# Pooling mixer: the mixer's weights first, on raw inputs, then the norm's scale, then the pooling

## The chip, the core and the metric

The kernel runs on one core of one Trainium2 chip. The metric is the device time of one execution in microseconds (us), the median of several runs. The core's engines are TensorE (PE in the profile, with PEld for its weight loads), VectorE (DVE), ScalarE (ACT), GpSimd (POOL), and SyncE (SP), which here issues the DMA transfers. Each works through its own queue in program order, and semaphores make one wait for another.

## The reference

A trunk of two layers on 512 tokens of 1024 features, in float32: pooling mixer, gated MLP, sliding-window attention, gated MLP, each behind an RMSNorm, with plain residual adds. The change is in the pooling mixer of layer 0, the first thing the kernel computes:

```python
def rms_norm(x, g):
    y = xf * lax.rsqrt(jnp.mean(xf * xf, axis=-1, keepdims=True) + RMS_EPS)
    return (y * g.astype(jnp.float32)).astype(x.dtype)

def pool_mixer(h, w, b, scale):
    csum = jnp.cumsum(hf, axis=1)
    for gi, win in enumerate(POOL_WINDOWS):          # 2, 4, 8, 16; 256 features each
        ...
        count = jnp.minimum(t1, win)
        mean = (c - lo) / count                       # causal mean over win tokens
        outs.append(mean - hf[..., sl])
    y = jnp.einsum('bsgc,gcd->bsgd', p, w) + b        # 256 x 256 weights a group
    return y.reshape(B, S, D) * scale

    h = h + mix                                       # then rms_norm and the gated MLP
```

## The kernel before

Tokens are handled in 4 tiles of 128 (`NT`), features in 8 chunks of 128 (`NC`), two chunks to each pooling window. In the residual `h` the features lie on the partitions and the 512 tokens along the row, one tile per chunk. PSUM has eight banks of 512 float32 columns. Products in nearly full precision are made of three fp32r matmuls (`mm3`, L84 to L86): an operand x is split into a rounded part, `x_h`, which ACT writes, and the rest, `x_l`, which DVE writes (`split_scaled`, L258 and L259, with a factor for each feature); weights are split in the same manner (L98 on ACT, L101 on DVE or POOL). A few matmuls take plain float32 operands.

The mixer comes in these steps:

1. SP loads the inputs token-major (`xt<-x_tok`, L145), the mixer's weights (L149), the vectors (L150), three weight tiles of the MLP (L90), and the inputs once more, feature-major, as `h` (L318).
2. TensorE multiplies zeros (`warm`, L270) while nothing has arrived.
3. For each token tile, ACT squares and sums the inputs (L288; for the first tile DVE does half, L277), a short chain on ACT and DVE gives the norm's factor for each token (`rsqrt_mean`, L193 to L211), and DVE multiplies the pooling band by it (`sband`, L297). The band is a small matrix, 128 x 144, that has 1/window in the places of the window and -1 more on the diagonal; the first tile has a variant for the first tokens (`edge`). Eight float32 matmuls (L299) then pool that tile, with the scale in the band, into eight banks, feature-major.
4. `mixed` (order letter m) splits each bank with the norm's gain into `px_h`, `px_l`; `product` (p) multiplies by the weights, 6 matmuls for each chunk; `bias` (b, L338) adds bias times scale to `h`; `total` (t, L341) adds the scaled product to `h`.
5. `normed` (n) splits `h` with the next norm's gain into `f0x_h` and `f0x_l`, the operands of MLP 0; `early_weights` (w) splits the MLP's first weight tiles, the l part on POOL in quarters; `norm.add` sums the squares of `h` (ACT L222, POOL L231) for the MLP's norm, whose statistics (`ones` against `n_acc`, L237) are used behind the first four weight tiles.

`pin` keeps what it wraps in program order on its engine; the order string near L348 sets that order for the last three groups of steps. The MLP begins with two weight tiles together: for each chunk k there are six matmuls, so that chunk k+1 is needed 6 matmuls after chunk k; then come two more tiles over all eight chunks, the second's statistics in between, and so on.

Of the kernel before, what the change touches and what calls it, by code (L numbers as in the profile page):

```python
# [54 lines left out]


@with_exitstack
def trunk(ctx: ExitStack, tc: tile.TileContext, x_tok, x_t, vecs, w_pool, w_kq, w_v, w_o, w_in, w_out, out_a, out_b):
    nc = tc.nc
    V, A, G, T = nc.vector, nc.scalar, nc.gpsimd, nc.tensor  # L60
    PSUM = bass.MemoryType.PSUM
# [7 lines left out]
    def small(pool, n, words, dt=F32, **kw):  # L69
        return pool.tile([P, words], dt, **kw)[:, :n]  # L70
# [76 lines left out]
    wpool_raw = [fst.tile([P, 1024], F32, name=f"wpool{g}_raw") for g in range(2)]  # L147
    for g in range(2):
        nc.sync.dma_start(wpool_raw[g], w_pool[:, g * 1024 : (g + 1) * 1024])  # L149
    nc.sync.dma_start(vec, vecs)  # L150
    h = [xp.tile([P, S], F32, tag="h", name=f"h{c}") for c in range(NC)]

    def col(i):
        return vec[:, i : i + 1]
# [2 lines left out]
    ident = cst.tile([P, P], F32, name="ident")  # L157
    make_identity(nc, ident)


    rc = small(fst, 16, 64, name="rc")
    for t in range(15):
        V.memset(rc[:, t : t + 1], 1.0 / (t + 1))
    band = fst.tile([P, 8, BW], F32, name="band")
    def edge_copy(g):
        a = WINDOWS[g] - 1
        pin(V.tensor_copy(band[:, 4 + g, a:], band[:, g, a:]))

    for g, w in enumerate(WINDOWS):
        b = band[:, g, :]  # L170
        V.memset(b, 1.0 / w)
        G.affine_select(b, b, [[1, BW]], ALU.is_ge, 0.0, base=0, channel_multiplier=-1)
        G.affine_select(b, b, [[-1, BW]], ALU.is_ge, 0.0, base=w - 1, channel_multiplier=1)
        G.affine_select(b, b, [[1, BW]], ALU.not_equal, 1.0 / w - 1.0, base=0, channel_multiplier=-1)
        f = band[:, 4 + g, : w - 1]
        G.affine_select(f, rc[:, : w - 1], [[1, w - 1]], ALU.is_ge, 0.0, base=0, channel_multiplier=-1)
        G.tensor_tensor(f, f, ident[:, : w - 1], ALU.subtract)
        if g < 2:
            edge_copy(g)
    ones = cst.tile([P, P], F32, name="ones")  # L180
    G.memset(ones, 1.0)


    def rsqrt_mean(dst, ssq, n, root=False):


        def tmp(k, dt=F32):
            return small(sm, n, 16, dt, tag=f"rs_{k}", name=f"rs_{k}", bufs=4)

        v = tmp("v")  # L190
        y = tmp("y")
        if root:
            A.activation(y, ssq, AF.Sqrt, bias=eps, scale=1.0 / D)  # L193
            pin(V.tensor_scalar(v, ssq, -0.5 / D, -0.5 * EPS, ALU.mult, ALU.add))
            pin(V.reciprocal(y, y))
        else:
            V.tensor_scalar(v, ssq, 1.0 / D, EPS, ALU.mult, ALU.add)
            sh = tmp("i", I32)
            V.tensor_scalar(sh, v.bitcast(I32), 1, None, ALU.logical_shift_right)
            V.tensor_scalar(y.bitcast(I32), sh, -1.0, float(0x5F3759DF), ALU.mult, ALU.add)  # L200
            V.tensor_scalar(v, v, -0.5, None, ALU.mult)
        t = tmp("t")
        steps = 1 if root else 3
        for it in range(steps):
            z = dst if it == steps - 1 else y
            if n == 1:
                V.scalar_tensor_tensor(t, y, y, v, ALU.mult, ALU.mult)
            else:
                V.tensor_tensor(t, y, y, ALU.mult)
                V.tensor_tensor(t, t, v, ALU.mult)  # L210
            V.scalar_tensor_tensor(z, t, 1.5, y, ALU.add, ALU.mult)  # L211
# [48 lines left out]
        return xh, xl  # L260


    def pool_mixer(norm, xs, ws):
        r0 = small(fst, NT, 32, name="r0")
        ss0 = small(fst, 2 * NT, 32, name="ss0")

        warm = small(fst, BW, 192, name="warm")
        V.memset(warm, 0.0)
        for i in range(12):
            T.matmul(banks[-1][:, :BW], lhsT=warm[:, :P], rhs=warm, start=True, stop=True)  # L270
        for i in range(NT):

            cut = D // 2 if i == 0 else D
            junk = fst.tile([P, D], F32, tag="junk", name=f"junk{i}")
            if cut < D:
                pin(
                    V.tensor_tensor_reduce(  # L277
                        out=junk[:, cut:],
                        in0=xt[:, i, cut:],
                        in1=xt[:, i, cut:],  # L280
                        scale=1.0,
                        scalar=0.0,
                        op0=ALU.mult,
                        op1=ALU.add,
                        accum_out=ss0[:, NT : NT + 1],
                    )
                )
            A.activation(junk[:, :cut], xt[:, i, :cut], AF.Square, accum_out=ss0[:, i : i + 1])  # L288
            if cut < D:
                pin(V.tensor_tensor(ss0[:, i : i + 1], ss0[:, i : i + 1], ss0[:, NT : NT + 1], ALU.add))  # L290
                for g in (2, 3):
                    edge_copy(g)
            rsqrt_mean(r0[:, i : i + 1], ss0[:, i : i + 1], 1, root=True)
            n = min(BW, S - i * P)
            sband = fst.tile([P, 4, BW], F32, tag="sband", name=f"sband{i}", bufs=2)
            e = 0 if i else 4
            pin(V.tensor_scalar(sband[:, :, :n], band[:, e : e + 4, :n], r0[:, i : i + 1], None, ALU.mult))  # L297
            for c in range(NC):
                T.matmul(  # L299
                    banks[c][:, i * P : i * P + n],  # L300
                    lhsT=xt[:, i, c * P : (c + 1) * P],
                    rhs=sband[:, c // 2, :n],
                    start=(i == 0),
                    stop=(i == NT - 1),
                    skip_group_check=True,
                )
        wpool = []
        for g in range(4):
            raw = wpool_raw[g // 2][:, (g % 2) * 512 : (g % 2 + 1) * 512]
            hh = fst.tile([P, 512], F32R, name=f"wpool{g}_h")  # L310
            ll = fst.tile([P, 512], F32R, name=f"wpool{g}_l")
            A.activation(hh, raw, AF.Copy)
            pin(V.tensor_tensor(ll, raw, hh.bitcast(F32), ALU.subtract))
            wpool.append((hh, ll))
        pre = [(0, 1), (0, 0), (1, 1), (1, 0)]
        raws = [fetch(w_in[0, j, t], D, f"wi0_{j}_{t}") for j, t in pre[:3]]
        for c in range(NC):
            nc.sync.dma_start(h[c], x_t[:, c, :])  # L318
        bs = small(cst, NC, 64, name="bs")
        pin(V.tensor_tensor(bs, vec[:, V_PB : V_PB + NC], vec[:, V_PS : V_PS + NC], ALU.mult))  # L320
        pool_x = {}

        def mixed(c):
            pool_x[c] = split_scaled(banks[c], col(V_NM + c), f"px{c}", pin)

        def early_weights(i):
            ws.append(in_weights(0, *pre[i], G, raws[i] if i < 3 else None, pin))

        def product(c):
            g = c // 2  # L330
            ps = bank("ps")
            for k in range(2):
                w = tuple(t[:, k * 256 + (c % 2) * P :][:, :P] for t in wpool[g])
                mm3(ps, w, pool_x[2 * g + k], k == 0, k == 1)
            return ps

        def bias(c):
            pin(A.activation(h[c], h[c], AF.Identity, bias=bs[:, c : c + 1]))  # L338

        def total(c):  # L340
            pin(V.scalar_tensor_tensor(h[c], ps[c], col(V_PS + c), h[c], ALU.mult, ALU.add))  # L341

        def normed(c):
            xs.append(split_scaled(h[c], col(V_NFF + c), f"f0x{c}", pin))


        ps = {}
        order = (  # L348
            "m0 m1 p0 p1 w0 m2 m3 p2 p3 b0 b1 t0 m4 m5 p4 p5 t1 b2 b3 t2 m6 m7 p6 p7 t3 w1 b4 b5 t4 t5 "
            "n0 b6 b7 t6 n1 t7 n2 w2 n3 n4 w3 n5 n6 n7"  # L350
        )
        for step in order.split():
            c = int(step[1])
            if step[0] == "p":
                ps[c] = product(c)
            else:
                {"m": mixed, "b": bias, "t": total, "n": normed, "w": early_weights}[step[0]](c)
        for c in range(NC):
            norm.add(c)

# [472 lines left out]
```

## Time and profile before

| | us |
|---|---|
| median of 3 runs (lowest, highest) | 927.53 (927.15, 928.12) |
| the profiled execution | 929.0 |
| its span, first to last instruction | 926.9 |
| TensorE busy in it | 913.3 |
| first matmul of MLP 0 | 27.52 |

The times of instructions below are counted from the start of the span. A row of a timeline has the start, the duration (from the start of the first to the end of the last where several are joined, "x6"), engine, line, operation, output<-inputs, shape and, in brackets, the idle time ahead of it with what ended it. A row of a group has the count and, behind the bar, busy us and mean ns of one, then the engine's idle time ahead. A row of one tile has the shortest, median and longest duration in ns, then the first and last start. A row of windows has its length, PE's busy time with the number of matmuls, the granted clock, the DMA engines' share and GB/s. Instructions next to each other on one engine overlap a little at their ends. One float32 matmul is two records.

### The profile page before, as it was taken

How to read it: one execution, taken by the hardware profiler on the slowest of the kernel's cores; microseconds unless marked ns; L12 is line 12 of the kernel's file. 1: busy time of each engine (PE TensorE's matmuls, PEld its weight loads, DVE VectorE, ACT ScalarE, POOL GpSimd, SP SyncE). 2: the span in 40 equal slices, each digit the busy share in tenths (PEclk: the TensorE clock that was granted, in tenths of full speed). 3: DMA queues.
4: the chain of work that ended last, by engine and by line, in shares of the span. 5: the costliest groups of instructions: out<-in, count | busy, mean ns of one | idle time of the engine just before them, and what ended most of it. 6: DMA issues, size and time to landing. Idle time of an engine off the chain costs nothing.

```text
span 926.9 us, 11709 instructions
## 1 busy us (share of the span) xinstructions
PE 913.3 (99%) x4419; PEld 769.2 (83%) x4419; DVE 577.8 (62%) x974; ACT 422.9 (46%) x682; POOL 132.6 (14%) x216
## 2 busy tenths in 40 slices
PE   8999999999999999999999999999999999999997
PEld 7888888888888888898888888888888888888896
DVE  6589766336777754455887472987743377677433
ACT  7765443223444443436887451744422244444532
POOL 3800000000000001217665040000000000000022
PEclk9999999999999999999999999999999999999999
DMA  8233222343222223322110041242233423322312
GB/s 332 71 113 114 94 84 79 94 128 113 92 91 95 75 77 101 130 91 91 47 46 24 20 140 52 85 152 92 63 94 100 136 91 94 109 80 64 94 62 91
DMA packets 28855, 88.13 MB, mean 95 GB/s; under 512 B 3200, under 2 KB 4352, under 8 KB 28800
## 3 DMA queue, kind: packets, MB, share of 16 engines
q1 hardware_dynamic: 28800, 87.40, 29.1%
q8 instruction: 34, 0.56, 0.2%
q14 instruction: 21, 0.17, 0.1%
HBM read 85.29 MB, written 2.10 MB: 94 GB/s over the span
## 4 chain that ended last, share of the span: by engine, by line
PE 88%; POOL 3%; ACT 3%; DVE 2%; issue 2%; DMA 1%; SPq 0%; ACTq 0%; POOLq 0%; DVEq 0%
PE bank L84 29%; PE bank L85 29%; PE bank L86 29%; POOL wi_l L101 2%; DMA wi_raw<-w_in 1%; ACT sc L625 1%; POOL n_acc L231 1%; PE bank L608 1%; PE bank L638 1%; POOL wo_l L101 0%; DVE q L521 0%; DVE tl L642 0%; PE bank L248 0%; DVE wi_l L101 0%; ACT th L641 0%
## 5 line engine op out<-in xcount | busy, mean ns | idle before, releaser
L98 ACT ACTIVATE wi_h<-wi_raw 128x1024 fp32r<-128x1024 f32 x88 | 93.0, 1060 | 102.0 <-PE bank L85 94.2
L231 POOL TENSOR_TENSOR n_acc<-n_acc,n_sq 128x512 f32<-128x512 f32 (+1 forms) x28 | 37.2, 1328 | 706.3 <-ACT n_sq L222 699.5
L84 PE MATMUL bank<-f0x_h,wi_h 128*128 128x512 f32 x352 | 137.2, 390 | 0.0
L85 PE MATMUL bank<-f0x_l,wi_h 128*128 128x512 f32 x352 | 137.2, 390 | 0.0
L84 PE MATMUL bank<-f1x_h,wi_h 128*128 128x512 f32 x352 | 137.1, 390 | 0.0
L84 PE MATMUL bank<-zh,wo_h 128*128 128x512 f32 (+1 forms) x363 | 137.0, 378 | 0.0
L86 PE MATMUL bank<-f0x_h,wi_l 128*128 128x512 f32 x352 | 137.0, 389 | 0.0
L86 PE MATMUL bank<-f1x_h,wi_l 128*128 128x512 f32 x352 | 136.9, 389 | 0.0
L85 PE MATMUL bank<-f1x_l,wi_h 128*128 128x512 f32 x352 | 136.9, 389 | 0.0
L86 PE MATMUL bank<-zh,wo_l 128*128 128x512 f32 (+1 forms) x363 | 136.6, 376 | 0.0
L85 PE MATMUL bank<-zl,wo_h 128*128 128x512 f32 (+1 forms) x363 | 136.6, 376 | 0.0
L101 DVE TENSOR_TENSOR wi_l<-wi_raw,wi_h 128x1024 fp32r<-128x1024 f32 x84 | 103.6, 1236 | 50.2 <-ACT wi_h L98 48.4
L98 ACT ACTIVATE wo_h<-wo_raw 128x768 fp32r<-128x768 f32 (+1 forms) x70 | 57.5, 823 | 121.8 <-PE bank L85 109.8
L365 DVE TENSOR_TENSOR c_u<-bank,n_rb 128x512 f32<-128x512 f32 x88 | 60.0, 687 | 76.6 <-PE bank L86 76.4
L101 DVE TENSOR_TENSOR wo_l<-wo_raw,wo_h 128x768 fp32r<-128x768 f32 (+1 forms) x66 | 60.3, 914 | 54.5 <-ACT wo_h L98 54.3
L85 PEld LDWEIGHTS bank<-zl,wo_h 128*128 128x128 f32 x363 | 68.3, 188 | 12.4
L84 PEld LDWEIGHTS bank<-zh,wo_h 128*128 128x128 f32 x363 | 68.3, 188 | 12.4
L86 PEld LDWEIGHTS bank<-zh,wo_l 128*128 128x128 f32 x363 | 68.3, 188 | 12.4
L85 PEld LDWEIGHTS bank<-f0x_l,wi_h 128*128 128x128 f32 x352 | 66.1, 188 | 14.6 <-DVE f0x_l L259 0.8
L85 PEld LDWEIGHTS bank<-f1x_l,wi_h 128*128 128x128 f32 x352 | 66.1, 188 | 13.8
L86 PEld LDWEIGHTS bank<-f1x_h,wi_l 128*128 128x128 f32 x352 | 66.1, 188 | 13.7
L84 PEld LDWEIGHTS bank<-f0x_h,wi_h 128*128 128x128 f32 x352 | 66.1, 188 | 13.7
(175 smaller groups left out, 1482.6 us busy)
## 6 DMA issues: line engine op xcount, KB each, us to landing
wi_raw<-w_in SPq DMA_DIRECT2D x88, 512.0 KB, 3.2
wo_raw<-w_out SPq DMA_DIRECT2D x31, 384.0 KB, 3.1
wo_raw<-w_out SPq DMA_DIRECT2D x31, 320.0 KB, 2.9
kq_raw<-w_kq SPq DMA_DIRECT2D x10, 512.0 KB, 3.2
wo_raw<-w_o SPq DMA_DIRECT2D x8, 512.0 KB, 3.2
xt<-x_tok SPq DMA_DIRECT2D x4, 512.0 KB, 5.2
h<-x_t SPq DMA_DIRECT2D x8, 256.0 KB, 8.6
wpool_raw<-w_pool SPq DMA_DIRECT2D x2, 512.0 KB, 8.4
```

The costliest lines, as they stand in the source:

```text
L84: T.matmul(ps, lhsT=wh, rhs=xh, start=start, stop=False, **kw)
L85: T.matmul(ps, lhsT=wh, rhs=xl, start=False, stop=False, **kw)
L86: T.matmul(ps, lhsT=wl, rhs=xh, start=False, stop=stop, **kw)
L98: pin(A.activation(h[:, :n], raw[:, :n], AF.Copy))
L101: (eng or V).tensor_tensor(l[:, o], raw[:, o], h[:, o].bitcast(F32), ALU.subtract)
L231: eng.tensor_tensor(self.acc[:, lo:hi], self.acc[:, lo:hi], sq[:, lo:hi], ALU.add)
L365: V.tensor_tensor(u, ps, rb, ALU.mult)
L608: T.matmul(o, lhsT=qt, rhs=kt[:, kk : kk + 256], start=x == 0, stop=x == 1)
L625: A.activation(t, t, AF.Exp, bias=neg[:, i : i + 1], scale=-1.0, accum_out=den[:, i : i + 1])
L638: T.transpose(ps[:, i * P : (i + 1) * P], sc[i // 2][:, i % 2, kb * P : (kb + 1) * P], ident)
```

## The change

Pooling (over tokens), the mixer's weights (over features) and the norm's scale (for each token) can be applied in another order. After the change the weights come first, on raw inputs:

- There is no token-major copy. SP loads `gm` (the norm's gain, 4 KB), then `h` and the weights in turns of 256 KB (lines 152 to 157 of the new program).
- `scaled` (w) multiplies the weights by the norm's gain on ACT and DVE. `mix` (y) multiplies, with the inputs as stationary operand, so the result has tokens on the partitions: y0 to y2 are 24 float32 matmuls of 256 columns, y3 is 24 fp32r matmuls of three-part products. They fill eight banks with two token tiles each, 256 columns for a tile.
- `square` (s) sums the squares on ACT and DVE; `scales` (r) gets all four factors by 4 float32 matmuls with `ones` and one scalar chain.
- `evict` (e) applies the factor to each token tile while it splits: `yh` on ACT, `yl` on DVE, 32 pieces of 256 columns. `pool` (c) multiplies these by the band in fp32r: 9 matmuls for each chunk, feature-major, into the same banks.
- `bias` of chunks 0 to 3 is done by POOL. `total` (L385) and `normed` (L268, L269) compute what they did.
- The order string is rewritten, and so is the order on the engines.

SP's queue at its start, before and now:

```order
-L145 DMA xt<-x_tok 128x1024 x4
-L149 DMA wpool_raw<-w_pool 128x1024 x2
-L150 DMA vec<-vecs 128x692
+L867 UNCONDITIONAL_BRANCH
+L152 DMA gm<-vecs 128x8
+L154 DMA h_95<-x_t 128x512
+L155 DMA wpool_raw<-w_pool 128x512
+L156 DMA h_96<-x_t 128x512
```

The four 512 KB tiles of the token-major input are gone, and `h`, which stood behind the third weight tile of the MLP, comes first.

VectorE from the last mixer operands to the MLP's operands. `h_96` to `h_103` are the eight chunks in before; this is before:

```order
L341 SCALAR_TENSOR_TENSOR h_99<-bank_73,vec,h_99 128x512
L341 SCALAR_TENSOR_TENSOR h_100<-bank_74,vec,h_100 128x512
L341 SCALAR_TENSOR_TENSOR h_101<-bank_75,vec,h_101 128x512
L259 SCALAR_TENSOR_TENSOR f0x_l<-h_96,vec,f0x_h 128x512
L341 SCALAR_TENSOR_TENSOR h_102<-bank_70,vec,h_102 128x512
L259 SCALAR_TENSOR_TENSOR f0x_l<-h_97,vec,f0x_h 128x512
L341 SCALAR_TENSOR_TENSOR h_103<-bank_71,vec,h_103 128x512
L259 SCALAR_TENSOR_TENSOR f0x_l<-h_98,vec,f0x_h 128x512
L259 SCALAR_TENSOR_TENSOR f0x_l<-h_99,vec,f0x_h 128x512
```

The totals (L341) stand several chunks ahead of the splits (L259). The same place of VectorE now, where the chunks are `h_95` to `h_102`:

```order
L385 SCALAR_TENSOR_TENSOR h_95<-bank_70,vec,h_95 128x512
L269 SCALAR_TENSOR_TENSOR f0x_l<-h_95,vec,f0x_h 128x512
L348 SCALAR_TENSOR_TENSOR yl_429<-bank_77,r_207,yh_428 128x256 x2
L348 SCALAR_TENSOR_TENSOR yl_429<-bank_76,r_207,yh_428 128x256 x2
L385 SCALAR_TENSOR_TENSOR h_96<-bank_71,vec,h_96 128x512
L269 SCALAR_TENSOR_TENSOR f0x_l<-h_96,vec,f0x_h 128x512
L385 SCALAR_TENSOR_TENSOR h_97<-bank_72,vec,h_97 128x512
L269 SCALAR_TENSOR_TENSOR f0x_l<-h_97,vec,f0x_h 128x512
```

The first total and split stand ahead of the last group's evictions, and then total and split take turns.

ScalarE in before, from the mixer's splits to the MLP's (L258 with a bank writes `px_h`, with `h` writes `f0x_h`):

```order
L258 ACTIVATE px_h<-bank_76,vec 128x512
L258 ACTIVATE px_h<-bank_77,vec 128x512
L98 ACTIVATE wi_0_0_h<-wi_0_0_raw 128x1024
L338 ACTIVATE h_100<-h_100,bs 128x512
L338 ACTIVATE h_101<-h_101,bs 128x512
L258 ACTIVATE f0x_h<-h_96,vec 128x512
L338 ACTIVATE h_102<-h_102,bs 128x512
L338 ACTIVATE h_103<-h_103,bs 128x512
L258 ACTIVATE f0x_h<-h_97,vec 128x512
```

ScalarE now, with the waits that each instruction carries (DVE_49 and PE_49 are the semaphores that VectorE and TensorE count up):

```order
L347 ACTIVATE yh_394<-bank_74,r_207 128x256
L347 ACTIVATE yh_394<-bank_74,r_207 128x256 [waits DVE_49]
L347 ACTIVATE yh_394<-bank_75,r_207 128x256 [waits PE_49]
L347 ACTIVATE yh_394<-bank_75,r_207 128x256 [waits DVE_49]
L268 ACTIVATE f0x_h<-h_95,vec 128x512 [waits DMAHW5_49,DVE_49]
```

Whole banks of 512 columns are replaced by halves, and the second half of a bank waits for VectorE.

The diff, cut to its core:

```diff
-    xt = fst.tile([P, NT, D], F32, name="xt")
-    for i in range(NT):
-        nc.sync.dma_start(xt[:, i, :], x_tok[i * P : (i + 1) * P, :])
+    for i in range(8):
+        T.matmul(banks[7][:, :BW], lhsT=warm[:, :P], rhs=warm, start=True, stop=True)
+    nc.sync.dma_start(gm, vecs[:, V_NM : V_NM + NC])
+    for g in range(4):
+        nc.sync.dma_start(h[2 * g], x_t[:, 2 * g, :])
+        nc.sync.dma_start(wpool_raw[g], w_pool[:, g * 512 : (g + 1) * 512])
+        nc.sync.dma_start(h[2 * g + 1], x_t[:, 2 * g + 1, :])
...
+        YB = (0, 1, 2, 3, 4, 5, 7, 6)
...
+        def square(c):
+            if c == 0:
+                pin(A.activation(acc, h[c], AF.Square))
+                return
+            sq = fst.tile([P, S], F32, tag="sq0", name=f"sq0_{c}", bufs=4)
+            pin(A.activation(sq, h[c], AF.Square))
+            pin(V.tensor_tensor(acc, acc, sq, ALU.add))
+        def mix(g):
+            g, half = divmod(g, 10)
+            for i in (2 * half, 2 * half + 1):
+                ps = banks[YB[2 * g + i // 2]][:, (i % 2) * 256 : (i % 2 + 1) * 256]
+                sl = slice(i * P, (i + 1) * P)
+                for k in range(2):
+                    c = 2 * g + k
+                    if g in ONE:
+                        mm3(ps, tuple(t[:, sl] for t in gx[c]), gw[g][k], k == 0, k == 1)
+                    else:
+                        T.matmul(ps, lhsT=h[c][:, sl], rhs=gw[g][k], start=k == 0, stop=k == 1)
+        def evict(g):
...
+            for i in range(NT):
+                ps = banks[YB[2 * g + i // 2]][:, (i % 2) * 256 : (i % 2 + 1) * 256]
+                c = r0[:, i : i + 1]
+                pin(A.activation(yh[g][:, i, :], ps, AF.Copy, scale=c))
+                pin(V.scalar_tensor_tensor(yl[g][:, i, :], ps, c, yh[g][:, i, :].bitcast(F32), ALU.mult, ALU.subtract))
+        def pool(c):
...
+                steps = [(y[g][:, i, o : o + P], b[:, g, :w]) for y in (yh, yl)]
+                if i == 0:
+                    steps.append((yh[g][:, i, o : o + P], edge_l[:, g, :]))
+                for y, m in steps:
+                    T.matmul(ps[c][:, i * P : i * P + m.shape[-1]], lhsT=y, rhs=m, ...)
...
-            "m0 m1 p0 p1 w0 m2 m3 p2 p3 b0 b1 t0 m4 m5 p4 p5 t1 b2 b3 t2 m6 m7 p6 p7 t3 w1 b4 b5 t4 t5 "
-            "n0 b6 b7 t6 n1 t7 n2 w2 n3 n4 w3 n5 n6 n7"
+            "w0 s0 s1 y0 y1 w1 s2 s3 y10 y11 w2 s4 s5 y20 w3 s6 s7 x6 x7 i0 r0 y21 y30 y31 b0 b1 b2 b3 "
+            "e0 c0 c1 e1 c2 c3 i1 e2 c4 c5 t0 n0 b4 e3 c6 c7 t1 n1 t2 n2 b5 t3 n3 b6 t4 n4 b7 t5 n5 t6 n6 i2 t7 n7 i3"
```

More of the change, by code (lines that the diff above doesn't have):

```diff
@@ L57, in trunk @@
 @with_exitstack
-def trunk(ctx: ExitStack, tc: tile.TileContext, x_tok, x_t, vecs, w_pool, w_kq, w_v, w_o, w_in, w_out, out_a, out_b):
+def trunk(ctx: ExitStack, tc: tile.TileContext, x_t, vecs, w_pool, w_kq, w_v, w_o, w_in, w_out, out_a, out_b):
     nc = tc.nc
@@ L158, in trunk @@
     make_identity(nc, ident)
+    ones = cst.tile([P, P], F32, name="ones")
+    G.memset(ones, 1.0)
     rc = small(fst, 16, 64, name="rc")
@@ L192, in rsqrt_mean @@
         if root:
-            A.activation(y, ssq, AF.Sqrt, bias=eps, scale=1.0 / D)
+            pin(A.activation(y, ssq, AF.Sqrt, bias=eps, scale=1.0 / D))
             pin(V.tensor_scalar(v, ssq, -0.5 / D, -0.5 * EPS, ALU.mult, ALU.add))
@@ L263, in pool_mixer @@
     def pool_mixer(norm, xs, ws):
[L264 to L314, printed above, removed]
+        ONE = (3,)
         pre = [(0, 1), (0, 0), (1, 1), (1, 0)]
         raws = [fetch(w_in[0, j, t], D, f"wi0_{j}_{t}") for j, t in pre[:3]]
-        for c in range(NC):
-            nc.sync.dma_start(h[c], x_t[:, c, :])
@@ new lines, in square, with split @@
+        def square(c):
[5 more added lines that the diff above has]
+            pin(V.tensor_tensor(acc, acc, sq, ALU.add))
+        def split(c):
+            hh = fst.tile([P, S], F32R, name=f"gxh{c}")
+            ll = fst.tile([P, S], F32R, name=f"gxl{c}")
+            pin(A.activation(hh, h[c], AF.Copy))
+            pin(V.tensor_tensor(ll, h[c], hh.bitcast(F32), ALU.subtract))
+            gx[c] = (hh, ll)
@@ new lines, in scales @@
+        def scales(_):
+            ps = banks[6]
+            for j in range(NT):
+                T.matmul(ps[:, 2 * j : 2 * j + 2], lhsT=acc[:, j * P : (j + 1) * P], rhs=ones[:, :2], start=True, stop=True)
+            rsqrt_mean(r0, ps[:, : 2 * NT].rearrange("p (a b) -> p a b", b=2)[:, :, 0], NT, root=True)
+        def evict(g):
+            yh[g] = fst.tile([P, NT, 256], F32R, name=f"yh{g}")
+            yl[g] = fst.tile([P, NT, 256], F32R, name=f"yl{g}")
+            for i in range(NT):
[3 more added lines that the diff above has]
+                pin(V.scalar_tensor_tensor(yl[g][:, i, :], ps, c, yh[g][:, i, :].bitcast(F32), ALU.mult, ALU.subtract))
@@ L326, in early_weights @@
         def early_weights(i):
             ws.append(in_weights(0, *pre[i], G, raws[i] if i < 3 else None, pin))
[L329 to L335, printed above, removed]
-        def bias(c):
-            pin(A.activation(h[c], h[c], AF.Identity, bias=bs[:, c : c + 1]))
+        def bias(c):
+            if c == 0:
+                V.tensor_tensor(bs, vec[:, V_PB : V_PB + NC], vec[:, V_PS : V_PS + NC], ALU.mult)
+            if c < 4:
+                G.tensor_scalar(h[c], h[c], bs[:, c : c + 1], None, ALU.add)
+            else:
+                pin(A.activation(h[c], h[c], AF.Identity, bias=bs[:, c : c + 1]))
```

85 lines of the change are left out of this document (58 added, 27 removed).

## The prediction

> **What bounds the kernel now.** I read the page's busy shares first, then TensorE (PE) in windows, then the timelines of the opening, since the rest of the program is left as it was.
>
> ```profile
> span 926.9 us, 11709 instructions
> PE 913.3 (99%) x4419; PEld 769.2 (83%) x4419; DVE 577.8 (62%) x974; ACT 422.9 (46%) x682; POOL 132.6 (14%) x216
> ...
> core 0: us, PE busy (x), PEclk, DMA share, GB/s
> 0.00:27.52 27.52, 23.99 (x136) 1.00 0.75 281
> 27.52:36.49 8.97, 8.97 (x39) 1.00 0.24 75
> 36.49:50.62 14.13, 14.13 (x69) 1.00 0.21 72
> ```
>
> 27.52 is the first matmul of MLP 0, 36.49 the end of the last f0x_l, 50.62 the first matmul after the statistics. From 27.52 on PE is busy all the time: nothing after the opening can absorb a delay, and whatever the opening loses is lost at the end. So I only have to find how late the same place (before: 50.62) is reached in the new program.
>
> ```profile
> 2.22 4.67 PE L270 MATMUL bank<-warm 128*128 128x144 f32 x24 [2.22 <-DVE warm L268]
> 7.66 7.93 PE L299 MATMUL bank<-sband,xt 128*128 128x144 f32 x64 [0.77 <-DVE rs_v L194]
> 21.91 0.50 PE L84 MATMUL bank<-px_h,wpool_h 128*128 128x512 f32 x1 [0.54 <-DVE px_l L259]
> ...
> 49.13 0.39 PE L84 MATMUL bank<-f0x_h,wi_h 128*128 128x512 f32 x1
> 49.35 0.39 PE L85 MATMUL bank<-f0x_l,wi_h 128*128 128x512 f32 x1
> 49.58 0.39 PE L86 MATMUL bank<-f0x_h,wi_l 128*128 128x512 f32 x1
> 49.81 0.95 PE L237 MATMUL bank<-ones,n_acc 128*128 128x2 f32 x8
> ...
> 25.06 2.06 DVE L341 SCALAR_TENSOR_TENSOR h<-bank,vec,h 128x512 f32<-128x512 f32 x3
> 27.04 0.74 DVE L259 SCALAR_TENSOR_TENSOR f0x_l<-h,vec,f0x_h 128x512 fp32r<-128x512 f32 x1
> ...
> 30.00 6.49 DVE L259 SCALAR_TENSOR_TENSOR f0x_l<-h,vec,f0x_h 128x512 fp32r<-128x512 f32 x6
> ...
> L341 DVE SCALAR_TENSOR_TENSOR h<-bank,vec,h 128x512 f32<-128x512 f32 x8 | 5.7, 742 | 1.6 <-ACT h L338 1.6
> ```
>
> The reader is to see three things. A float32 matmul of 128 or 144 columns is two records, and 64 of them take 7.93: 0.124 each. A 512-wide fp32r matmul comes every 0.23. And VectorE (DVE) does six splits f0x_l in a row in 6.49, because the totals (L341) they need were done ahead: there the splits cost 1.08 a chunk and PE, which consumes a chunk in 6 matmuls (6 x 0.23 = 1.4), never waits long.
>
> **The opening of the changed program, stage by stage.**
>
> *Stage A, to the scale r0.* The new PE stream begins with matmuls on raw inputs.
>
> ```profile
> 4.22 0.63 ACT L288 ACTIVATE junk<-xt 128x512 f32<-128x512 f32 x1 [1.93 <-DMA xt<-x_tok]
> 5.54 1.06 ACT L288 ACTIVATE junk<-xt 128x1024 f32<-128x1024 f32 x1
> 12.29 1.15 ACT L312 ACTIVATE wpool_h<-wpool_raw 128x512 fp32r<-128x512 f32 x2 [0.57 <-DMA wpool_raw<-w_pool]
> ...
> L222 ACT ACTIVATE n_sq<-h 128x512 f32<-128x512 f32 x7 | 4.3, 631 | 6.9 <-POOL n_acc L231 6.9
> L313 DVE TENSOR_TENSOR wpool_l<-wpool_raw,wpool_h 128x512 fp32r<-128x512 f32 x4 | 2.5, 685 | 0.0
> ...
> 10.38 0.29 ACT L193 ACTIVATE rs_y<-ss,eps 128x1 f32<-128x1 f32 x1
> 10.71 0.16 DVE L195 RECIPROCAL rs_y<-rs_y 128x1 f32<-128x1 f32 x1
> 11.16 0.16 DVE L211 SCALAR_TENSOR_TENSOR r<-rs_t,rs_y 128x1 f32<-128x1 f32 x1
> ```
>
> The first 0.5 MB landed at 4.2 and the first 1 MB by 5.5; h0, its weights and h1 are 0.75 MB behind one 4 KB transfer (gm), so both inputs of the first product are there between 4.2 and 5.5. I take 4.7, plus 0.3 for the weight scaling: 5.0. Ahead of r0 stand 22 float32 matmuls of 256 columns, two records each; the L299 row by width gives 0.124 x 256/144 = 0.22 a record, so 22 x 0.44 = 9.7, with 0.4 for waits on arrivals 10.1, to 15.1. The warm row shows a slow start: 24 records in 4.67 instead of 24 x 0.124 = 3.0. With 16 warm records instead of 24 the slow stretch may fall on real work: 0 to +1.7, nearest 0 since the first real matmul starts late enough. Statistics are 8 records as in the L237 row, 0.95, to 16.05; the scalar chain took 10.38 to 11.32 on one column and has one operation more (0.2) and two waits: 1.45. r0 is there at 17.5. The squares and their adds are hidden: in before 3 MB had landed at 12.3 (the L312 row), as many as the new inputs and weights have, and the last square and add, 0.63 and 0.69, end near 13.7, ahead of the statistics at 15.1.
>
> *Stage B, 32 evictions.* The scale now rides on evictions of 256 columns: yh on ScalarE (ACT), then yl on VectorE, two column halves in each of 8 banks.
>
> ```profile
> L657 ACT ACTIVATE oh<-bank x16: 359/375/387, 447.6 to 524.3; 128x256 fp32r<-128x256 f32 x16
> L641 ACT ACTIVATE th<-bank x28: 577/592/605, 442.9 to 520.9; 128x512 fp32r<-128x512 f32 x28
> L258 ACT ACTIVATE px_h<-bank,vec 128x512 fp32r<-128x512 f32 x8 | 5.0, 682 | 0.6 <-PE bank L299 0.6
> L533 DVE SCALAR_TENSOR_TENSOR vv<-bank,n_r,vec x4: 484/484/485, 415.1 to 422.0; 128x256 f32<-128x256 f32 x4
> L98 ACT ACTIVATE wi_h<-wi_raw 128x1024 fp32r<-128x1024 f32 x12 | 12.6, 1056 | 7.7 <-DVE rs_t L209 2.8 <-PE bank L85 2.6 <-DMA wi_raw<-w_in 2.2
> ```
>
> yh: 0.375, plus 0.09 for the column scale (682 less 592): 0.46. yl: 0.484. In the built program the second yh of a bank waits for VectorE's yl of the first half, so a bank is yl, signal, yh, signal, yl: 0.48 + 0.04 + 0.46 + 0.04 + 0.40 = 1.42. A signal is the gap from ACT's rs_y, 10.38 + 0.29 = 10.67, to the reciprocal at 10.71; 0.40 is 0.48 less 0.08, since operations in a row overlap so much (three totals of 0.74 in 2.06). The next bank's first yh lies beside the last yl. Eight banks: 11.4. Put in between on the same engines: wi_h of the second weight tile, 1.06 on ACT less its overlap, +0.9; then t0, f0x0_h and a bias, 0.74 + 0.72 + 0.72 with two signals and a wait less an overlap, +2.6. The first yl starts at 17.5 + 0.5 = 18.0; 18.0 + 11.4 + 0.9 + 2.6 = 32.9. The 72 pooling matmuls stand between evictions: at 0.07, 0.12 or 0.25 a piece (a narrow fp32r price is not in the trace; by width from the 512 row 0.07, and a whole float32 matmul of two records 0.25 bounds it from above; I take half of that, 0.12, so 1.1 a chunk against 1.42 a bank) they trail the evictions; only the last 9 count, +0 to +1.1, and t1 doesn't wait for them. I cost them at nothing; cover: the gaps of the evictions. The same covers the 24 fp32r products of group 3, which run while group 0 is evicted.
>
> *Stage C, totals and splits.* VectorE's order is t1 n1 t2 n2 ... t7 n7. n needs f0x_h on ACT, which needs t: nothing runs ahead any more.
>
> ```profile
> L258 ACT ACTIVATE f0x_h<-h,vec 128x512 fp32r<-128x512 f32 x8 | 5.3, 721 | 0.0
> L259 DVE SCALAR_TENSOR_TENSOR f0x_l<-h,vec,f0x_h x8: 740/1110/1227, 27.0 to 35.3; 128x512 fp32r<-128x512 f32 x8
> 30.28 8.21 POOL L101 TENSOR_TENSOR wi_l<-wi_raw,wi_h 128x256 fp32r<-128x256 f32 x8 [1.91 <-ACT wi_h L98]
> 38.44 9.53 POOL L231 TENSOR_TENSOR n_acc<-n_acc,n_sq 128x512 f32<-128x512 f32 x7
> ```
>
> A chunk is 0.74 + 0.04 + 0.72 + 0.04 + 0.74 less 0.08 of overlap = 2.20; seven: 15.4. The last f0x_l ends at 32.9 + 15.4 = 48.3 (before 36.49). PE needs 1.4 a chunk and gets one every 2.2: it starves here. The splits at 1110 stand beside GpSimd's (POOL) wi_l. POOL now has n_acc and wi_l in this stretch too, 6 x 1.3 + 4 x 0.74 = 10.8 of 15.4, so a split may be 0 to 0.49 longer (1227 less 740): 0 to +3.4 in all. In the steady beat n_acc starts after f0x_h's square and lies mostly beside the total; I take +0.5, to 48.8.
>
> [...]
>
> *Stage D, to the place compared.* In before 14.13 lay between the last f0x_l and 50.62. PE still has the second pair of tiles then, 48 x 0.23 = 11.0, some 4 products of chunk 7, 0.9, and the statistics, 0.9: 12.8. Its last weight tile is split by ACT after f0x7_h and by POOL in quarters, 1.06 + 0.74: +0.4 of waiting. 48.8 + 13.2 = 62.0, plus 0.1 for the first matmul after a wait (21.91: 0.50 instead of 0.39), against 50.62: **+11.5**.
>
> What is removed: 8 records of warming, 32 pooling matmuls in float32 (7.9), 48 products (48 x 0.23 = 11.0), their evictions px, 2 MB of token-major transfers, three of four rsqrt chains. All of it is in the stages above by being absent from them; the new start is simply the sum A to D. SP's queue: 17 issues up to the third weight tile and h, where 18 stood, 2 MB less; wi_raw lands earlier, hidden, since by the sum the second tile is asked for at 23.7 (18.0 and four banks). POOL rounds the bands into fp32r tables and adds four biases: hidden, as the pooling matmuls begin after 19 and the first total comes at 28.
>
> **Sum against the profiled execution:** span 926.9 + 11.5 = 938.4, and with the 2.1 that lie outside the span (929.0 in all) 940.5. The median of the runs is 927.53, 1.5 under that execution; the difference carried over gives 927.5 + 11.5 = **939.0**.
>
> **Rivals.**
>
> Evictions overlap: ACT and VectorE read different halves of one bank without taking turns. Then VectorE paces a bank at 2 x 0.40 = 0.81 instead of 1.42, 8 x 0.61 = 4.9 less: 934.1. For it: no row of before shows such a wait (oh and ol meet once a bank). Against: the wait is in the built program.
>
> [...]
>
> Other side, faster: PE stays the bound, as it is from 27.52 in before. By PE alone, with narrow fp32r by width (256 columns 0.12, the pooling 0.07, from 0.23 for 512), the steady MLP starts at 5.0 + 10.1 + 0.9 + 24 x 0.12 + 72 x 0.07 = 23.9 against 27.52: 3.6 less, 923.9; at 0.12 a pooling matmul 27.5 and no change. For it: 99% busy. Against: it decides only if evictions, totals and splits from r0 on end by 36; that is 18.5 where the rows add up to 31.
>
> Worse: every split at 1227 (+3.4 in place of +0.5) and the slow start on real work (+1.7): 943.6. For it: six of eight splits in before were slow. Against: the beat above.
>
> No change: the program's start is later, but f0x chunks suffice for PE, as in before. It needs stage C at 1.4 a chunk and B at 0.81 a bank: 7 x 0.8 + 4.9 = 10.5 of the 11.5 goes, leaving +1.0 (928.5). Nothing speaks for both.
>
> **Chances.** Forecast 0.77; overlap 0.08; worse 0.08; faster 0.04; no change 0.03. Range: from under the overlap (934.1, less 3.1 for an r0 up to 2 earlier and the slack of the other terms) to above the worse (943.6), 931 to 945; left out is 0.07 and the tails. A measurement of this kernel tells 0.2% (1.9) from no change: faster 0.04, same 0.03, slower 0.93.
>
> **What would show it.** After: r0's last operation near 17.5; yl rows in pairs with ACT's second yh starting behind the first yl, 1.4 a bank; last yl near 33; then VectorE alternating totals and splits, 2.2 a chunk, with PE waiting for f0x_h and f0x_l; last f0x_l near 49; the first matmul after L237's kind near 62; after it PE as before. Wrong I would be if yl rows are continuous, or if PE shows no waits between 34 and 49, or if the span shows a gain after 62.

## The result, and the profile after

The changed kernel takes 943.5 us in the median of 4 executions (942.27 to 946.75), beside 927.72 for the kernel before in as many: 1.0175 times as long, 95% interval 1.0161 to 1.0189 (the medians alone give 1.0170). By the medians that is 15.8 more; forecast were 939.0, 11.5 more, with a range of 931 to 945. The profiled execution took 943.2, its span is 941.5, so the profile has 14.6 of it. Of all executions below one is far off: the kernel with all three edits and zeros took 2399.78 once, where its three others took 937.17 to 937.84, and its ratio leaves that one out.

First the page's shares and then windows of TensorE in the changed kernel, cut where the stages end; the columns are those of before.

```profile
span 941.5 us, 11804 instructions
PE 925.3 (98%) x4451; PEld 779.8 (83%) x4451; DVE 578.4 (61%) x971; ACT 423.7 (45%) x686; POOL 141.1 (15%) x232
...
21.02:27.41 6.39, 4.81 (x39) 0.98 0.22 66
27.41:32.01 4.60, 4.60 (x19) 0.50 0.39 140
32.01:40.58 8.57, 7.83 (x29) 0.50 0.00 1
40.58:49.72 9.14, 9.09 (x39) 0.99 0.01 2
49.72:53.98 4.26, 1.77 (x9) 1.00 0.36 123
53.98:57.61 3.63, 3.63 (x10) 0.57 0.17 33
57.61:66.05 8.44, 8.44 (x43) 0.98 0.45 172
66.05:91.62 25.57, 25.57 (x119) 1.00 0.20 62
```

The reader is to see the clock column: it stands at 0.50 from 27.41 to 40.58 and falls again at 53.98, each time behind a stretch in which TensorE ran dry (idle for 1.58 of the 6.39 ahead of 27.41, and for 2.49 ahead of 53.98). In the windows of before it was 1.00 throughout. The place that the prediction compares, the first matmul behind the statistics, is at 66.05 (before 50.62; forecast 62.0): 15.4 later. From there to the end the changed kernel needs 875.4, before 876.3: it gains 0.8 back. TensorE has no idle time in the 25.6 us behind that place, where before had 0.66 (busy 24.91 of 25.57).

Now the timelines of the changed kernel, stage by stage: TensorE's start, the scale r0, the evictions of VectorE and of ScalarE, and the totals and splits.

```profile
5.37 1.22 PE L332 MATMUL bank<-gw,h 128*128 128x256 f32 x2
7.26 9.30 PE L332 MATMUL bank<-gw,h 128*128 128x256 f32 x42 [0.66 <-DMA h<-x_t]
16.40 0.95 PE L337 MATMUL bank<-ones,n_acc 128*128 128x2 f32 x8
18.46 0.16 DVE L221 SCALAR_TENSOR_TENSOR r<-rs_t,rs_y 128x4 f32<-128x4 f32 x1
19.16 0.48 DVE L348 SCALAR_TENSOR_TENSOR yl<-bank,r,yh 128x256 fp32r<-128x256 f32 x1 [0.54 <-ACT yh L347]
19.68 0.84 ACT L347 ACTIVATE yh<-bank,r 128x256 fp32r<-128x256 f32 x2 [0.55 <-DVE yl L348]
20.19 0.88 DVE L348 SCALAR_TENSOR_TENSOR yl<-bank,r,yh 128x256 fp32r<-128x256 f32 x2 [0.54 <-ACT yh L347]
21.10 0.84 ACT L347 ACTIVATE yh<-bank,r 128x256 fp32r<-128x256 f32 x2 [0.58 <-DVE yl L348]
21.61 0.88 DVE L348 SCALAR_TENSOR_TENSOR yl<-bank,r,yh 128x256 fp32r<-128x256 f32 x2 [0.54 <-ACT yh L347]
33.55 0.48 DVE L348 SCALAR_TENSOR_TENSOR yl<-bank,r,yh 128x256 fp32r<-128x256 f32 x1 [0.54 <-ACT yh L347]
33.95 0.74 DVE L385 SCALAR_TENSOR_TENSOR h<-bank,vec,h 128x512 f32<-128x512 f32 x1
34.72 0.72 ACT L268 ACTIVATE f0x_h<-h,vec 128x512 fp32r<-128x512 f32 x1 [1.21 <-DVE h L385]
35.48 0.75 DVE L269 SCALAR_TENSOR_TENSOR f0x_l<-h,vec,f0x_h 128x512 fp32r<-128x512 f32 x1 [0.79 <-ACT f0x_h L268]
36.15 0.74 DVE L385 SCALAR_TENSOR_TENSOR h<-bank,vec,h 128x512 f32<-128x512 f32 x1
48.95 0.77 DVE L269 SCALAR_TENSOR_TENSOR f0x_l<-h,vec,f0x_h 128x512 fp32r<-128x512 f32 x1 [0.79 <-ACT f0x_h L268]
```

yl pairs start at 20.19 and 21.61: 1.42 a bank, and in each bank ACT waits for VectorE 0.55 to 0.58 and VectorE for ACT 0.54. Totals start at 33.95 and 36.15: 2.20 a chunk. The last f0x_l ends at 49.72. Then the end of the opening, on POOL, VectorE and TensorE:

```profile
47.74 3.29 POOL L101 TENSOR_TENSOR wi_l<-wi_raw,wi_h 128x256 fp32r<-128x256 f32 x4 [1.29 <-ACT wi_h L98]
50.99 1.27 POOL L241 TENSOR_TENSOR n_acc<-n_acc,n_sq 128x512 f32<-128x512 f32 x1
52.23 1.70 POOL L101 TENSOR_TENSOR wi_l<-wi_raw,wi_h 128x256 fp32r<-128x256 f32 x1
51.53 1.81 DVE L101 TENSOR_TENSOR wi_l<-wi_raw,wi_h 128x1024 fp32r<-128x1024 f32 x1 [1.80 <-ACT wi_h L98]
51.10 0.39 PE L85 MATMUL bank<-f0x_l,wi_h 128*128 128x512 f32 x1
53.98 0.50 PE L86 MATMUL bank<-f0x_h,wi_l 128*128 128x512 f32 x1 [2.49 <-POOL wi_l L101]
54.62 0.63 PE L86 MATMUL bank<-f0x_h,wi_l 128*128 128x512 f32 x1
55.05 0.63 PE L84 MATMUL bank<-f0x_h,wi_h 128*128 128x512 f32 x1
```

POOL gets to the fourth weight tile at 52.23, behind the third tile and a sum. Its first quarter, for which TensorE waits, then takes 1.70, while the eight quarters of the two tiles take 0.74 in the median. VectorE's work on the tile after these (51.53 to 53.34) lies beside it and is long as well: 1.81, where the 84 of its kind in the whole profile take 1.24 in the mean. TensorE stands idle for 2.49, and the matmuls after that start 0.43 apart (54.62 to 55.05) where they start 0.23 apart at the full clock.

### The profile page after: what moved, and what is told of

Same layout as the page of the kernel before. It is cut to its first block, busy times and chain, and to the rows that moved or that the text cites. A ratio compares the mean times of both kernels' runs of the same rounds, so it can differ in the third digit from the quotient of the medians.

```text
span 941.5 us, 11804 instructions
## 1 busy us (share of the span) xinstructions
PE 925.3 (98%) x4451; PEld 779.8 (83%) x4451; DVE 578.4 (61%) x971; ACT 423.7 (45%) x686; POOL 141.1 (15%) x232
## 4 chain that ended last, share of the span: by engine, by line
PE 90%; ACT 4%; DVE 3%; POOL 1%; issue 1%; DMA 1%; SPq 0%; ACTq 0%; POOLq 0%; DVEq 0%
PE bank L84 29%; PE bank L85 29%; PE bank L86 29%; ACT sc L665 1%; PE bank L332 1%; PE bank L648 1%; PE bank L678 1%; DVE yl L348 1%; ACT f0x_h L268 1%; ACT yh L347 1%; DVE h L385 1%; DMA h<-x_t 1%; POOL wi_l L101 0%; POOL wo_l L101 0%; DVE q L561 0%
## 5 line engine op out<-in xcount | busy, mean ns | idle before, releaser
L86 PEld LDWEIGHTS bank<-f0x_h,wi_l 128*128 128x128 f32 x352 | 66.9, 190 | 16.9 <-POOL wi_l L101 2.9
```

The costliest lines, as they stand in the source:

```text
L86: T.matmul(ps, lhsT=wl, rhs=xh, start=False, stop=stop, **kw)
```

## The experiments

My theory after this profile: the prediction's chains (turns within a bank, turns of total and split) are what costs, and what I lacked is the wait for POOL and the slow clock behind it. Rival: TensorE's half clock from 27 to 41 is the missing part, or paces the whole stretch. Times are medians of 4 executions, ratios are to the kernel before. A difference to the changed kernel is that of the ratio to 1.0175, which comes out up to 0.6 us larger than by the medians. Where the profiles are compared, "the place" is the first matmul behind the MLP's statistics, and I count it from r0 (the end of the L221 row), since r0 comes between 18.6 and 20.75 in these profiles: 66.05 - 18.62 = 47.4 in the changed kernel.

### Another bank with every piece

```diff
-            for i in range(NT):
+            for i in (0, 2, 1, 3):
```

> One edit: the four pieces of each eviction group go in the order of token tiles 0, 2, 1, 3, so that ACT and VectorE change bank with every piece; the same instructions otherwise. Theory (the two halves of a bank take turns and that costs 0.6 a bank): VectorE paces the pieces at 0.41 in place of 0.71 on average, the last yl ends near 29.2 in place of 34.0, and the time falls by 4.8 to about 938.5. Rival (the pooling matmuls at the low granted clock, 1.9 us a chunk, pace this stage): last pooling matmul stays at 36 to 37 and the time falls by less than 1. Rival (nothing but the chain of totals and splits counts): the same 4.8, since that chain only starts earlier, but then it must show in t1's start.

939.66, ratio 1.0125 (1.011 to 1.014): 4.6 less by the ratios. VectorE's timeline in this run:

```profile
20.32 1.66 DVE L348 SCALAR_TENSOR_TENSOR yl<-bank,r,yh 128x256 fp32r<-128x256 f32 x4 [0.15 <-ACT yh L347]
...
30.20 0.74 DVE L385 SCALAR_TENSOR_TENSOR h<-bank,vec,h 128x512 f32<-128x512 f32 x1
```

Four pieces now take 1.66, 0.4 each, and the first total of the chain of seven starts at 30.20 in place of 33.95. The place is at 60.93. The same instructions in another order lose the turns within a bank, so these are shown to cost time. How much is read from r0, which is at 18.75 here: the last f0x_l ends 27.2 behind it (45.97) in place of 31.1, so the turns cost 3.9 and not the 4.9 of the sum. The place comes 42.2 behind r0, 5.2 earlier. The other 1.4 lies behind TensorE's wait for POOL: this ends 3.9 earlier too (50.24), is 1.65 long in place of 2.49, and the clock stays at 1.00 behind it. That the time fell by nearly the forecast amount is luck in part.

### Totals ahead of splits

The end of the order string:

```diff
-e3 c6 c7 t1 n1 t2 n2 b5 t3 n3 b6 t4 n4 b7 t5 n5 t6 n6 i2 t7 n7 i3
+e3 c6 c7 t1 t2 n1 b5 t3 n2 b6 t4 n3 b7 t5 n4 t6 n5 t7 n6 i2 n7 i3
```

> One edit: the tail of the order takes each total one chunk ahead of the split (t1 t2 n1 t3 n2 ...), as the kernel before did, and the last two weight tiles keep their places behind n6 and n7. Theory (the alternation t, f0x_h, f0x_l costs 0.8 a chunk): VectorE does a chunk in 1.4 in place of 2.2, the last f0x_l ends near 44.4 in place of 49.7; the last weight tile's POOL part starts 5 earlier with it. Then the time falls by about 5, to 938.5. Rival (PE at the low granted clock until 40.6 is the bound of this stretch by itself): the first 48 MLP matmuls end at 49 instead of 50, so the end moves by 1 from the splits and by up to 4 from the vanished wait for the weight tile: 938.5 to 942.5, with the last f0x_l early but PE without idle time from 37 on.

939.57, ratio 1.0123 (1.0106 to 1.014), 4.8 less. Here r0 came at 20.0, 1.4 later than in the profile above, and still the last f0x_l ended at 46.7:

```profile
38.20 0.74 DVE L269 SCALAR_TENSOR_TENSOR f0x_l<-h,vec,f0x_h 128x512 fp32r<-128x512 f32 x1
38.86 0.74 DVE L385 SCALAR_TENSOR_TENSOR h<-bank,vec,h 128x512 f32<-128x512 f32 x1
39.52 0.74 DVE L269 SCALAR_TENSOR_TENSOR f0x_l<-h,vec,f0x_h 128x512 fp32r<-128x512 f32 x1
45.62 1.08 DVE L269 SCALAR_TENSOR_TENSOR f0x_l<-h,vec,f0x_h 128x512 fp32r<-128x512 f32 x1 [0.62 <-ACT f0x_h L268]
```

The chunks of the first three rows take 1.32 without idle time; the last splits are longer, and the last one waits 0.62. From r0 the last f0x_l ends after 26.7 in place of 31.1, so the turns of total and split are worth 4.4 in the chain (5.3 forecast). The place is 62.00 - 20.00 = 42.0 behind r0, 5.4 less. What each part is worth in the time, though, isn't shown. The two readings can't be told apart by this time alone: TensorE had no idle time from 35 on in this run (its clock at 0.50 until about 41, then full), and the wait for POOL was gone as well.

### The last two weight tiles early

The end of the order string again:

```diff
-t1 n1 t2 n2 b5 t3 n3 b6 t4 n4 b7 t5 n5 t6 n6 i2 t7 n7 i3
+t1 n1 i2 t2 n2 i3 b5 t3 n3 b6 t4 n4 b7 t5 n5 t6 n6 t7 n7
```

> One edit: the weight tiles 3 and 4 of the MLP are split behind n1 and n2 in place of n6 and n7. PE then doesn't wait 2.5 for POOL at 51.5. Theory (the idle time also lowers the granted clock for the next 3.6 us, 8 matmuls at 0.43 in place of 0.23): the time falls by 2.5 + 1.6 = 4.1 less up to 0.6 for ACT's two earlier operations, to about 939.5 to 940, and there is no stretch at a clock near 0.5 between 50 and 60. Rival (only the wait counts): 2.5, to 941. Rival (the wait was covered by something else): no change, 943.5.

940.21, ratio 1.0135 (1.012 to 1.015), 3.7 less. But the profile is none that the theory describes: the wait is gone and others came, since POOL now had the weights before its sums, and ACT's squares for these waited for POOL ahead of the f0x_h behind them, 2.39 at 48.12.

```profile
46.17 0.74 DVE L385 SCALAR_TENSOR_TENSOR h<-bank,vec,h 128x512 f32<-128x512 f32 x1
...
49.42 0.74 PE L84 MATMUL bank<-f0x_h,wi_h 128*128 128x512 f32 x2 [1.04 <-ACT f0x_h L268]
```

The total of 46.17 got its split only at 49.40. The run shows that the wait can be moved, not what it cost.

### The fourth tile's rest on VectorE

```diff
-            ws.append(in_weights(0, *pre[i], G, raws[i] if i < 3 else None, pin))
+            ws.append(in_weights(0, *pre[i], G if i < 3 else None, raws[i] if i < 3 else None, pin))
```

> The changed kernel with one edit: the l part of the MLP's fourth weight tile is made by VectorE, which is free after the last split at 49.7, in place of POOL, which still has a sum and starts it at 52.2. Theory (the wait of 2.5 for POOL at 51.5, and the slow clock of the 8 to 10 matmuls behind it, are the main part of what the prediction lacked): the tile is there by 51.5, no idle time of TensorE over 0.6 and no slow stretch between 50 and 60, 3 to 4 less, to 940. Rival (only the wait counts, the clock falls anyway): 2 to 2.5 less, 941.2, with matmuls at 0.43 near 54. Rival (something else is late next, as in the run with the weights early): 0 to 1 less.

939.43 (939.36 to 939.7), ratio 1.0128 (1.0113 to 1.0143): 4.4 less, and this edit touches nothing ahead of 49.

```profile
50.74 1.51 DVE L101 TENSOR_TENSOR wi_l<-wi_raw,wi_h 128x1024 fp32r<-128x1024 f32 x1 [0.17 <-ACT wi_h L98]
...
50.00:54.00 4.00, 4.00 (x19) 1.00 0.05 10
54.00:58.00 4.00, 4.00 (x19) 1.00 0.90 323
```

In the windows of TensorE from 50 to 58 there is no idle time and the clock is at 1.00. r0 is at 19.45 here, and the place at 62.55: 43.1 behind r0, 4.3 less than 47.4. The wait of 2.49 doesn't explain that by itself; with the slow matmuls (3.63 for what 9 x 0.23 = 2.1 would take: 1.6) it is 4.1. From r0 to the end of the last f0x_l the two kernels take the same 31.1, so the gain lies behind it. This run is decisive for the wait and the slow clock together; POOL's queue and VectorE's work beside it both go with the edit, and it doesn't tell them apart.

### TensorE kept busy

Zeros are added to finished banks, so that TensorE doesn't run dry between evictions; in the changed kernel, and in the one with the first three edits of order together ("all three", with its own expectation first).

```diff
+            for _ in range({1: 2, 3: 5, 5: 12}.get(c, 0)):
+                T.matmul(ps[c][:, :BW], lhsT=warm[:, :P], rhs=warm, start=False, stop=True, skip_group_check=True)
```

> The changed kernel, with matmuls on zeros added to finished banks (2 behind chunk 1's pooling, 5 behind chunk 3's, 12 behind chunk 5's), so that TensorE isn't idle between the evictions; results are unchanged since zeros are added. Theory (the granted clock falls to a half by 27.4 because TensorE runs dry, but this is hidden, since ACT and VectorE pace the splits until 49.7): the stretch 27 to 41 shows a clock near 1.0 and pooling matmuls at 0.11, and the time stays within 1 of 943.5. Rival (the slow clock is part of what the prediction lacked): 2 to 4 less, 939.5 to 941.5. Third possibility (the added work itself delays chunks 4 to 7): 1 to 2 more.

943.65, ratio 1.0175 (1.0158 to 1.0192): no change. Windows of TensorE in this run:

```profile
27.00:32.00 5.00, 4.81 (x40) 1.00 0.57 203
32.00:41.00 9.00, 8.65 (x50) 1.00 0.01 3
41.00:50.00 9.00, 7.65 (x24) 1.00 0.00 0
```

The clock stays at 1.00, and the last f0x_l ends 31.1 behind r0 (50.20 - 19.09), as in the changed kernel: the low clock from 27 to 41 was hidden behind the chains, and the rival of 2 to 4 less falls. One thing the profile has that the median doesn't show:

```profile
54.45 0.50 PE L86 MATMUL bank<-f0x_h,wi_l 128*128 128x512 f32 x1 [1.64 <-POOL wi_l L101]
...
54.45:58.00 3.55, 3.54 (x15) 1.00 0.11 28
```

The wait for POOL ends 35.4 behind r0 in both kernels, but here it is 1.64 long and the clock stays at 1.00 behind it, where it fell behind 2.49. The place comes 46.1 behind r0 in place of 47.4, so the slow matmuls behind the wait cost 1.3 by these two profiles, and four executions of each are too few to see that in the time.

> The three edits together. Theory: last yl near 29, last f0x_l near 39.5, PE's first 48 MLP matmuls end near 43, the next 48 and the statistics near 54.5 in place of 66.0: 11.5 less than 943.5, 932, still above the kernel before by 4 since r0 comes at 18.6 and VectorE's 32 pieces, 8 totals and 8 splits alone take 13 + 5.3 + 5.4 = 23.7 behind it. Rival (PE at the low clock for 13 us): 935 to 937. Rival (terms hide each other): no better than the best of the three alone.

All three edits: 935.79, ratio 1.0086 (1.0071 to 1.0101), 8.3 less, not the 11.5 of the theory. The last f0x_l ended at 44.1, not 39.5.

```profile
37.63 1.26 DVE L269 SCALAR_TENSOR_TENSOR f0x_l<-h,vec,f0x_h 128x512 fp32r<-128x512 f32 x1
39.47 1.25 DVE L269 SCALAR_TENSOR_TENSOR f0x_l<-h,vec,f0x_h 128x512 fp32r<-128x512 f32 x1
```

VectorE's splits take 1.25 here (1.11 in the median of before, 1.23 at most). POOL's weight parts lie beside them (33.19 to 40.17), as they did in before; and TensorE, at half the clock until 39 (0.50 from 30 to 35, 0.53 from 35 to 40), had no idle time from 30.5 on. To tell these apart, the same with zeros (3 behind chunk 3, 11 behind chunk 5):

> The kernel with all three edits of order, with zeros added in the same manner (3 behind chunk 3's pooling, 11 behind chunk 5's). There TensorE has no idle time from 32 on and runs at half the clock until 39. Theory (in this kernel the low clock is what sets the end): the first 48 MLP matmuls end some 3 to 4 earlier and the time falls by 3 to 4, to about 932. Rival (VectorE's splits, slowed beside POOL, set the end as well, their last at 44): 1 less at most, 935.

937.52, ratio 1.0104 (1.0087 to 1.0121): 1.7 more by the ratios, not less, though the intervals overlap. The clock was full (MLP matmuls 0.23 apart from 33.6 on), and TensorE then waited for the splits. Why is in ACT's timeline:

```profile
38.94 1.14 ACT L232 ACTIVATE n_sq<-h 128x512 f32<-128x512 f32 x2
42.48 0.63 ACT L232 ACTIVATE n_sq<-h 128x512 f32<-128x512 f32 x1 [2.41 <-POOL n_acc L241]
43.02 0.71 ACT L268 ACTIVATE f0x_h<-h,vec 128x512 fp32r<-128x512 f32 x1
```

A square that has no hurry waits 2.41 for POOL's sum, and f0x_h stands behind it on ACT. Both theories had left this queue out.

### The squares behind the splits

The squares pinned on ACT behind the last f0x_h, in the kernel with all three edits and the zeros, and without the zeros:

```diff
-            A.activation(sq[:, lo:hi], h[c][:, lo:hi], AF.Square)
+            self.pin(A.activation(sq[:, lo:hi], h[c][:, lo:hi], AF.Square))
...
+        norm.pin = pin
```

> The kernel with the three edits of order and the zeros, and one more: the squares for the MLP's norm are pinned on ACT behind the last f0x_h. Without that edit they stood between the f0x_h on ACT and waited for POOL's sums (2.41 and 1.23), and the last f0x_l ended at 47.7 although TensorE ran at the full clock. Theory (that queue on ACT is what replaced the alternation): f0x_h are no longer held up, the last f0x_l ends near 42, the first 48 MLP matmuls end near 45, and the time falls by 3 to 4 from 937.5, to 934. Rival (VectorE's splits beside POOL's weights, 1.1 to 1.26 each, hold as much): 936 to 937.

> The same without the zeros, so TensorE goes idle for 2.4 before chunk 6 and falls to half the clock until 39. Theory (where the chain of splits is short, the low clock sets the end): last f0x_l near 42 as well, but the first 48 MLP matmuls end near 48 to 49, as they did without the late squares; the time stays at 935 to 936, 1.5 to 2.5 above the run with zeros. Rival (the clock never matters here): equal to the run with zeros.

934.58 with zeros, ratio 1.0076 (1.006 to 1.0092), 2.6 under the same kernel without the late squares; 934.85 without zeros, ratio 1.0081 (1.0064 to 1.0098). The last f0x_l ended at 43.0 with zeros, where it was 47.7: the queue on ACT was the hold-up there. Without zeros it moved from 44.1 to 42.6, and that time can't be told from 935.79. The place is 37.1 behind r0 with zeros and 38.7 without, 1.6 later (1.5 to 2.5 were forecast for the time), with the clock back at full speed by 36.3 (matmuls 0.23 apart behind it, 0.43 ahead) and not at 39; but the two times can't be told apart. What the clock is worth in the time stays open.

These are the fastest versions I tried, 7 us above the kernel before. From r0, about 19, VectorE alone has 32 pieces of 0.40, 8 totals and 8 splits of 0.66 at the least, 23.4 in all, so that its last split can't end before 42 as long as VectorE has all of these, where before's ended at 36.5. That this floor is what remains is an estimate; no run moved work off VectorE there.

### The start

```diff
-    for i in range(8):
+    for i in range(14):
```

> The changed kernel with 14 matmuls on zeros ahead of the first real one in place of 8. Theory (the slow start of TensorE falls on the first real matmuls in some executions, up to 2 us, and scatters r0 between 18.6 and 20.5): r0 at 18.5 to 19.2, the scatter between executions smaller, the median 0 to 1 lower, 942.5 to 943.5. Rival (arrivals of the inputs scatter, not the clock): the same 943.5 and the same scatter of 4 us.

943.58 (942.27 to 943.83), ratio 1.0167 (1.0152 to 1.0183). The scatter is smaller, 1.6 in place of 4.5, but four executions each don't settle that; the median is the same. In the profile no slow record is left among the first products, yet r0 comes at 19.40: the statistics wait 0.69 for VectorE's sum of squares.

```diff
-    nc.sync.dma_start(gm, ...)
+    nc.scalar.dma_start(gm, ...)
```

> The changed kernel with the 4 KB transfer of the norm's gain issued by ACT in place of SP, so that the inputs are issued 0.45 earlier. Theory (the first products wait for h1, which lands at 7.1 since all transfers under way share the rate): h1 lands 0.3 to 0.5 earlier, the time falls by as much at most, 943. Rival (the small transfer of 128 short pieces holds up the queue): h1 lands 1.5 or more earlier and the time falls by 1.5.

942.44, ratio 1.0159 (1.0143 to 1.0174). Earlier issue of 0.45 brought the products behind h1 to 6.51 in place of 7.26, but r0 wasn't earlier (its last operation started at 18.46 in both): the statistics waited 0.27 for the sum of squares. No effect is shown.

## Why the prediction was right, and where it fell short

The direction, the mechanism and the range held; the size was 4.5 short by the medians. Of these 3.1 lie in the span (941.5 where 938.4 was forecast). The other 1.4 come from carrying a profiled execution over to the median: before's profiled execution lay 1.5 above its median and had 2.1 outside the span, the changed kernel's lay 0.3 below and had 1.7. By its steps:

- **Stage A**, r0 at 17.5: it came at 18.62, 1.1 late. h1 landed at 7.1, not by 5.5, so the products behind it began at 7.26; from there they ran without a wait, and the statistics began at 16.40 (15.1 forecast), while what follows them took 0.2 less. The slow start fell on the first two records (1.22 for 2, at 0.22 each 0.44), but this 0.8 lay ahead of h1 and cost nothing here. In other profiles r0 came as late as 20.75: there three records behind h1 took 1.62. And in several the statistics waited for the sum of squares, by 0.69 at most, which I had called hidden.
- **Stage B**, 1.42 a bank, 15.4 from r0 to the last yl: measured 1.42 and 34.03 - 18.62 = 15.4. The wait within a bank was in the trace as it was in the program: ACT waits 0.55 to 0.58 for VectorE. It falls to 0.19, once in four pieces, when neighbouring pieces lie in different banks (all three edits), and the first experiment shows a price of 3.9 for it, where I had 4.9.
- **Stage C**, 2.20 a chunk and 0.5 for POOL: measured 2.20 in the row and 15.7 from last yl to last f0x_l (15.9 forecast). The splits took 0.75 to 0.88. The 1.23 each of the rival didn't come: POOL's sums lay mostly beside the totals and VectorE's waits (41.13 to 42.42 between a total from 40.68 and a split from 42.21).
- **Stage D**, 13.2, is the step that failed: measured 66.05 - 49.72 = 16.3. I gave the wait for POOL's part of the last tile 0.4, from its own length. I didn't count what stands ahead of it in POOL's queue (the third tile at 0.82 a quarter, and a sum), nor what lies beside it (the quarter of 1.70 in place of 0.74). The wait was 2.49. And I priced TensorE at the full clock there: 1.3 to 1.6 more behind the wait. Without these the kernel takes 939.4. That this is nearly the forecast 939.0 is luck in part: in that run stage D took 12.0 (62.55 - 50.58), 1.2 less than the 13.2 of the sum, which makes up for the late r0.
- **The clock.** I took it as 1.00 throughout, because before shows nothing else. It fell at 27.4, behind 6.4 us with 1.6 idle, and again behind 2.49 of idle time. The longest idle stretch ahead of 27.4 was 1.10, and the return took until 40.6, with one gap of 0.74 on the way; behind the second wait it took 3.6. With zeros in the gaps of the changed kernel it stayed at 1.00 from 27 to 50. Which gaps halve it isn't settled. Behind 2.46, 2.49 and 2.51 at the wait for POOL (14 warming matmuls, the changed kernel, the gain issued by ACT) the clock fell; behind 1.64 and 1.65 (zeros, banks in turn) it stayed at 1.00. And with all three edits and zeros it stayed full from 40 to 50 (matmuls 0.23 apart), with TensorE busy 7.24 of the 10 us and idle for 1.00 at most at a time.
- **After the place**: nothing forecast, 0.8 gained, which hides as much of the late stages.

Of the rivals, overlap, no change and faster are refuted by the turns in the rows. The worse one came nearest to the time (943.6) by another way: of its two terms the slow splits didn't come, and the slow start lay inside a wait.

## What to carry to other kernels

When a chain passes to and fro between two engines, its pitch was here the sum of both and the signals (1.42 a bank, 2.20 a chunk), and the order of the same instructions decided: change bank with every piece (3.9 off the chain), and take the next chunk's first step ahead of this chunk's last (4.4 off). For a stage that waits, price every item that stands ahead of the one waited for in its engine's queue, not the item alone; a square without hurry ahead of a needed split on ACT cost 2.4 here, a sum ahead of a needed weight on POOL over 1. Look beside the item too: VectorE's work next to POOL's needed quarter came with nearly 1 more. And a wait of TensorE is to be priced with the slow matmuls behind it, if nothing else hides these: 2.5 idle cost 4.1 to 4.4, while behind 1.6 there were none.

## What the runs showed of the hardware

Narrow fp32r matmuls, which the trace of before lacked, start 0.11 apart at 144 columns and 0.12 at 256 with the full clock, and 0.21 at 144 with half of it (28.52 and 28.73 in the changed kernel); pairs of rows of the changed kernel show the first two.

```profile
20.78 0.28 PE L85 MATMUL bank<-gwl,gxh 128*128 128x256 f32 x1
20.90 0.28 PE L86 MATMUL bank<-gwh,gxl 128*128 128x256 f32 x1
21.54 0.28 PE L363 MATMUL bank<-band,yh 128*128 128x144 f32 x1
21.65 0.27 PE L363 MATMUL bank<-band,yl 128*128 128x144 f32 x1
15.13 7.04 POOL L380 TENSOR_SCALAR h<-h,bs 128x512 f32<-128x512 f32 x4 [5.95 <-ACT gxh L317]
```

The 144 columns cost nearly as much as 256 here, 0.11 beside 0.12. And POOL's biases, the last row, took 1.76 each, the first of them 2.41, while VectorE was at its splits and the first evictions; nothing waited for them.
